# Twenty of the 64 chunks of w_down as seven block products in place of eight, and the transposes of q two half-chunks later

## The chip, the core and the metric

The kernel runs on one NeuronCore of a Trainium2 chip. The metric is the time of one execution on the device in microseconds (us); the median of three runs is compared. One further execution was recorded by the profiler.

TensorE multiplies matrices: it loads a 128x128 block as weights, streams up to 512 columns past it and adds the product to a bank of PSUM (eight banks of 128x512 fp32). VectorE and ScalarE work on tiles in SBUF and PSUM, GpSimd on tiles in SBUF. SyncE (SP) issues transfers. Each engine has a queue of its own and works through it in order; an instruction waits for the others by semaphores.

## What is computed

One decoder layer over 256 tokens of width 2048, in float32: a wide projection, a gated linear recurrence and sliding-window attention side by side, a mix, and a feed-forward part:

```
h = rmsnorm(x, norm_mix);  z = h @ w_in                  # 2048 x 9472
o_hg = hgrn2(...);  o_at = swa_sinks(rmsnorm(q), rmsnorm(k), v, sinks)
x = x + (sigmoid(g_hg) * (o_hg @ w_hg_out) + sigmoid(g_at) * (o_at @ w_at_out)) @ w_out
h2 = rmsnorm(x, norm_ffn)
x = x + square(relu(h2 @ w_up)) @ w_down                 # w_up 2048 x 8192, w_down 8192 x 2048
```

The change concerns the last product, and the transposes of the attention's q.

## The kernel before

All weights are read once, in 234 chunks of 1 MB (128 partitions x 16 x 128 values). A chunk `raw` is cut into two halves. A half is one *tick* of the program's main loop, so chunk i has the ticks 2i and 2i+1. For the accuracy of float32, each half is split into a rounded part `hi` (ScalarE's cast, `split_hi`) and the remainder `lo` (VectorE's subtraction, `split_lo`), and the activations are stored split in the same way. TensorE forms three products, of `hi` with `hi`, of `hi` with `lo` and of `lo` with `hi`.

The loop's order is the order of each engine's queue. At tick t it issues the cast of the half t+3, the remainder of the half t+2, the work that results due at t (`due`), then TensorE's matmuls of the half t, then what a table of ticks puts behind them (`post` for VectorE, ScalarE and GpSimd, `pe_side` for TensorE). A load is issued three chunks ahead. There are four buffers for `raw`, four for `hi` and three for `lo`.

The feed-forward part runs in two halves of D_FF. In each, 32 chunks of w_up give the activations `u0` and `u1` (16 tiles of 128 features x 256 tokens each, held as weights for the next product), and then 32 chunks of w_down follow. For w_down, a group of 8 chunks makes 512 columns of the output: `mm_tok` has 12 matmuls of 512 columns for each half chunk, six into the bank of the first 128 tokens and six into that of the other 128. `add_tok` then adds both banks to `x2`, which is the result; in the second half of D_FF it is written out at once.

`psm` and `pss` are two pools of four PSUM banks each. w_up and w_down use `psm`; `pss` holds small side results.

For q, `queries(b, tick)` takes one half of the heads: at `tick` it squares and sums (`a`), at tick+2 VectorE scales q (`a2`, the instruction written as aq<-aq,qsm, L714), at tick+3 TensorE makes eight transposes (`turn`, L724), at tick+4 ScalarE copies them out (`out`). The first half of q has tick 76, so its transposes stand behind the matmuls of tick 79. At tick 78, `post` also holds VectorE's products of the last recurrence group (L461, L462, L465), issued ahead of `a2`.

Of the kernel before, what the change touches and what calls it, by code (L numbers as in the profile page):

```python
# [18 lines left out]
P = 128  # L19
# [23 lines left out]
def trunk_kernel(  # L43
# [46 lines left out]
    rstd = base.tile([P, T], F32, name="rstd")  # L90
    keep = base.tile([P, T], F32, name="keep")
    consts = base.tile([P, C_W], F32, name="consts")
# [5 lines left out]
    sm = base.tile([P, 4, 2], F32, name="sm")  # L98
    qsm = base.tile([P, 3, 16], F32, name="qsm")
    base.tile([P, 232], F32, name="pad")  # L100

# [8 lines left out]

    raw_of, hi_of, lo_of = {}, {}, {}

    def load(i):
# [4 lines left out]
    def split_hi(h):  # L118
        i, q = divmod(h, 2)
        if N_START <= i < S_END:  # L120
            hi = hi_of[h] = split.tile([P, 8, P], F32R, tag="hi", bufs=4, name=f"hi{h}")
            nc.scalar.copy(hi, raw_of[i][:, 8 * q : 8 * q + 8, :])  # L122

    def split_lo(h):
        i, q = divmod(h, 2)
        if N_START <= i < S_END:
            lo = lo_of[h] = split.tile([P, 8, P], F32R, tag="lo", bufs=3, name=f"lo{h}")
            nc.vector.tensor_sub(lo, raw_of[i][:, 8 * q : 8 * q + 8, :], hi_of[h].bitcast(F32))  # L128
# [31 lines left out]
    def mm_tok(ps, act, k0, hi, lo, first, last):  # L160
        hi, lo = (w.rearrange("p (k a) b -> p k (a b)", k=2) for w in (hi, lo))
        for t in range(2):
            tok = slice(t * P, (t + 1) * P)
            for k in range(2):
                xh, xl = (act[:, k0 + k, a, tok] for a in range(2))
                nc.tensor.matmul(ps[t], lhsT=xh, rhs=hi[:, k, :], start=(first and k == 0), stop=False)  # L166
                nc.tensor.matmul(ps[t], lhsT=xh, rhs=lo[:, k, :], start=False, stop=False)  # L167
                nc.tensor.matmul(ps[t], lhsT=xl, rhs=hi[:, k, :], start=False, stop=(last and k == 1))  # L168

    def psum_main(i):  # L170
# [182 lines left out]
    def to_hgrn():  # L353
# [3 lines left out]
        for t in hg["aT"]:  # L357
            nc.gpsimd.memset(t, 0.0)
        nc.gpsimd.memset(keep, 1.0)
        nc.gpsimd.memset(keep.rearrange("p (c r) -> p c r", c=4)[:, :, 0:1], 0.0)  # L360
# [14 lines left out]
    def group(g):  # L375
# [55 lines left out]
        def post_scan():  # L431
            for i in range(2):
                v = st["lf"][:, i, :]
                nc.vector.tensor_tensor_scan(v, keep, v, 0.0, ALU.mult, ALU.add)  # L434

# [255 lines left out]
    def queries(b, tick):  # L691
# [10 lines left out]
        def a():  # L702
            sq = hg["pool"].tile([P, 16, 64], F32, tag="aqs", name=f"aqs_{b}")
            nc.scalar.activation(sq, heads(), AF.Square)
            v, r, t = st["small"] = [qsm[:, k, :] for k in range(3)]
            nc.vector.tensor_reduce(v.unsqueeze(2), sq, AX.X, ALU.add)
# [27 lines left out]
        at_post(tick + 2, a2)  # L734
        at_pe(tick + 3, turn)
        at_post(tick + 4, out)

# [161 lines left out]
    def open_ff():  # L899
# [5 lines left out]
        acts["h2"] = p.tile([P, KT, 2, T], F32R, name="h2")  # L905
        gp["sq"] = p.tile([P, 512], F32, name="sqt")
        gp["ss"] = p.tile([P, 2, 4], F32, name="ss")
        gp["r2"] = p.tile([P, 2], F32, name="r2")
# [52 lines left out]
    at_post(2 * S_FF + 4, lambda: norm_post("2"))  # L961

    def evac_up(k):
        box = {}
# [5 lines left out]
        def q(ps, n):  # L970
            nc.scalar.activation(box["s"], box["s"], AF.Square)  # L971
            split_act(acts[f"u{k // 16}"][:, k % 16], box["s"], nc.gpsimd.tensor_copy)

        return [(1, 0, f), (1, 1, q)]

    def evac_down(n, half):
        def f(ps, i):
            add_tok(ps, n)
            if half == 1:
                for t in range(2):  # L980
                    cols = slice(512 * n, 512 * n + 512)
                    nc.sync.dma_start(out[t, :, cols], gp["x2"][:, t, cols])

        return [(1, 0, f)]

# [16 lines left out]
    for half in range(2):  # L1002
        for k in range(32):
            jobs.append(("one", lambda: acts["h2"], evac_up(k)))
        for n in range(4):
            for c in range(8):
                jobs.append(
                    (
                        "tok",
                        lambda c=c: acts[f"u{c // 4}"],  # L1010
                        evac_down(n, half) if c == 7 else None,
                        4 * (c % 4),
                        c == 0,
                        c == 7,
                    )
                )
    assert len(jobs) == S_END
# [16 lines left out]
    for tick in range(2 * S_END + 2):  # L1034
# [10 lines left out]
        if tick == 2 * S_OUT + 3:  # L1045
            open_ff()
        split_hi(ticks[tick + 3])
        split_lo(ticks[tick + 2])
        for f in due.pop(tick, ()):
# [14 lines left out]
        elif i < S_END:  # L1064
            kind, act, ef = jobs[i][:3]
            if kind == "tok":
                k0, first, last = jobs[i][3:]
# [56 lines left out]
def _layout(inputs):  # L1124
# [39 lines left out]
    w_mix = np.concatenate([g["w_hg_out"].reshape(1024, D), g["w_at_out"].reshape(1024, D)[perm]], axis=0)  # L1164
    w_down = g["w_down"].reshape(2, D_FF // 2, D)
    w_down_t = np.concatenate([_rows(w_down[0]), _rows(w_down[1])], axis=0)
    cst, csr = _constants()
# [29 lines left out]
```

## Time and profile before

| | us |
|---|---|
| median of 3 runs (1353.06 to 1354.23) | 1353.5 |
| profiled execution, its own time | 1351.39 |
| its span, first to last instruction | 1349.6 |
| TensorE busy in it | 1336.0 |
| VectorE busy | 829.5 |
| ScalarE busy | 681.2 |
| GpSimd busy | 153.5 |

Busy time counts the stretches in which an engine has an instruction under way. Matmuls overlap, so the length of one is longer than the distance from one to the next. "Idle before" names the engine and line whose instruction ended the wait.

### The profile page before, as it was taken

Reading aid. Unit: us, or ns where it says so; the run is one execution under the profiler, and the core shown is the slowest. Engines: PE = TensorE matmul, PEld = TensorE weight load, DVE = VectorE, ACT = ScalarE, POOL = GpSimd, SP = SyncE. Lnnn points to the kernel's source line nnn. Section 1 sums busy time; section 2 is a strip of 40 time slices with the busy share of each in tenths; the row PEclk is TensorE's granted clock in tenths of the full one; section 3 lists DMA queues with packets and bytes.
Section 4 is the critical chain, followed back from the end, with each engine's and each line's share of the span. In section 5 each row is a group of like instructions: output and inputs, shape, how many; then the busy total and the mean of one; then the engine's idle time right before and its main releaser. Section 6 shows DMA issues by size and latency. Waiting matters only on the chain.

```text
span 1349.6 us, 17486 instructions
## 1 busy us (share of the span) xinstructions
PE 1336.0 (99%) x6776; PEld 1129.6 (84%) x6776; DVE 829.5 (61%) x989; ACT 681.2 (50%) x960; POOL 153.5 (11%) x163
## 2 busy tenths in 40 slices
PE   8999999999999999999999999999999999999998
PEld 7888888788888888888888888888888888888887
DVE  5767797676565567655766665444456666644443
ACT  7756576565666644454544444334344444433332
POOL 0332453100000001000000000000001111100000
PEclk9999999999999999999999999999999999999999
DMA  9655545455444555655555555555555555556661
GB/s 355 224 194 172 185 160 187 148 177 180 162 168 170 179 189 179 246 184 176 192 191 193 193 192 194 187 190 196 200 193 188 188 188 187 187 188 211 216 212 47
DMA packets 43331, 255.38 MB, mean 189 GB/s; under 512 B 4336, under 2 KB 10096, under 8 KB 13808
## 3 DMA queue, kind: packets, MB, share of 16 engines
q1 hardware_dynamic: 43104, 254.23, 54.9%
q8 instruction: 53, 0.87, 0.3%
q14 instruction: 30, 0.25, 0.0%
q10 hardware_dynamic: 144, 0.03, 0.0%
HBM read 252.15 MB, written 2.10 MB: 188 GB/s over the span
## 4 chain that ended last, share of the span: by engine, by line
PE 94%; DVE 2%; ACT 1%; issue 1%; DMA 1%; POOL 0%; SPq 0%; DVEq 0%; ACTq 0%; POOLq 0%
PE mm L136 23%; PE mm L166 19%; PE mm L167 19%; PE mm L168 19%; PE mm L145 12%; DVE lo L128 1%; DMA raw<-w_in_t 1%; PE pt L808 0%; PE po L823 0%; DVE lf L434 0%; PE s L754 0%; ACT hi L122 0%; PE o L530 0%; PE tr L931 0%; PE mt L884 0%
## 5 line engine op out<-in xcount | busy, mean ns | idle before, releaser
L128 DVE TENSOR_TENSOR lo<-raw,hi 128x1024 fp32r<-128x1024 f32 x460 | 582.1, 1268 | 421.5 <-PE mm L167 270.6
L122 ACT CAST hi<-raw 128x1024 fp32r<-128x1024 f32 x460 | 483.0, 1052 | 604.7 <-PE mm L168 380.3
L136 PE MATMUL mm<-h,hi 128*128 128x512 f32 x1024 | 305.9, 392 | 0.0
L136 PEld LDWEIGHTS mm<-h,hi 128*128 128x128 f32 x1024 | 187.9, 188 | 37.5
L145 PE MATMUL mm<-h,lo 128*128 128x256 f32 x1024 | 214.8, 281 | 0.0
L167 PE MATMUL mm<-lo,u 128*128 128x512 f32 x512 | 199.2, 389 | 0.0
L168 PE MATMUL mm<-hi,u 128*128 128x512 f32 x512 | 199.2, 389 | 0.0
L166 PE MATMUL mm<-hi,u 128*128 128x512 f32 x512 | 199.2, 389 | 0.0
L145 PEld LDWEIGHTS mm<-h,lo 128*128 128x128 f32 x1024 | 166.6, 190 | 5.0
L166 PE MATMUL mm<-hi,hT 128*128 128x512 f32 x384 | 152.7, 398 | 0.0
L167 PE MATMUL mm<-lo,hT 128*128 128x512 f32 x384 | 150.0, 391 | 0.7 <-DVE lo L128 0.7
L168 PE MATMUL mm<-hi,hT 128*128 128x512 f32 x384 | 149.6, 390 | 0.0
L167 PEld LDWEIGHTS mm<-lo,u 128*128 128x128 f32 x512 | 96.1, 188 | 20.1
L166 PEld LDWEIGHTS mm<-hi,u 128*128 128x128 f32 x512 | 96.1, 188 | 19.9
L168 PEld LDWEIGHTS mm<-hi,u 128*128 128x128 f32 x512 | 96.1, 188 | 19.8
L131 POOL CAST u<-s 128x256 fp32r<-128x256 f32 x64 | 44.1, 689 | 578.0 <-ACT s L971 578.0
L136 PE MATMUL mm<-hT,hi 128*128 128x512 f32 x352 | 88.4, 393 | 0.0
L166 PEld LDWEIGHTS mm<-hi,hT 128*128 128x128 f32 x384 | 72.2, 188 | 15.4 <-issue 1.4
L168 PEld LDWEIGHTS mm<-hi,hT 128*128 128x128 f32 x384 | 72.1, 188 | 15.4
L167 PEld LDWEIGHTS mm<-lo,hT 128*128 128x128 f32 x384 | 72.2, 188 | 14.8 <-DVE lo L128 1.1
L136 PEld LDWEIGHTS mm<-hT,hi 128*128 128x128 f32 x352 | 63.5, 189 | 11.6
L145 PEld LDWEIGHTS mm<-hT,lo 128*128 128x128 f32 x352 | 47.9, 190 | 4.2 <-DVE lo L128 0.8
(201 smaller groups left out, 1271.4 us busy)
## 6 DMA issues: line engine op xcount, KB each, us to landing
raw<-w_in_t SPq DMA_DIRECT2D x73, 1024.0 KB, 4.9
raw<-w_up_t SPq DMA_DIRECT2D x64, 1024.0 KB, 4.9
raw<-w_down_t SPq DMA_DIRECT2D x64, 1024.0 KB, 4.9
raw<-w_mix_t SPq DMA_DIRECT2D x16, 1024.0 KB, 4.9
raw<-w_out_t SPq DMA_DIRECT2D x16, 1024.0 KB, 4.9
xs<-x_tok SPq DMA_DIRECT2D x2, 1024.0 KB, 15.9
x<-x_tok SPq DMA_DIRECT2D x8, 256.0 KB, 6.4
out<-x SPq DMA_DIRECT2D x8, 256.0 KB, 2.8
```

The lines of the kernel that those rows point to most:

```text
L122: nc.scalar.copy(hi, raw_of[i][:, 8 * q : 8 * q + 8, :])
L128: nc.vector.tensor_sub(lo, raw_of[i][:, 8 * q : 8 * q + 8, :], hi_of[h].bitcast(F32))
L131: copy(dst[..., 0, :], src)
L136: nc.tensor.matmul(ps, lhsT=hi[:, k, :], rhs=act[:, k0 + k, :, :].rearrange("p a t -> p (a t)"), start=(first and k == 0), stop=False,)
L145: nc.tensor.matmul(ps[:, T : 2 * T], lhsT=lo[:, k, :], rhs=act[:, k0 + k, 0, :], start=False, stop=(last and k == hi.shape[1] - 1),)
L166: nc.tensor.matmul(ps[t], lhsT=xh, rhs=hi[:, k, :], start=(first and k == 0), stop=False)
L167: nc.tensor.matmul(ps[t], lhsT=xh, rhs=lo[:, k, :], start=False, stop=False)
L168: nc.tensor.matmul(ps[t], lhsT=xl, rhs=hi[:, k, :], start=False, stop=(last and k == 1))
```

## The change

Two blocks of 128 features and two of 512 output columns make a 2x2 problem: A11, A12, A21, A22 are the blocks of the activations (token half by feature block of 128) and B11, B12, B21, B22 those of w_down (feature block by 512 columns). The layout of w_down is changed on the host, so that one chunk holds the four B blocks, and a group is now 16 chunks that make 1024 columns. In five chunks of each group (0, 3, 6, 9 and 12; 20 of 64) the product is made by seven block products (Strassen's scheme, in the form with 4 sums of A and 4 of B), each of three matmuls; in the other chunks by eight, also three matmuls each (`mm_four`).

* A's sums are made while w_up is worked (`sums_up`), on 128x128 blocks.
* B's sums are made by VectorE in place, in `raw` (`seven_sums`), after the first half's `hi` and `lo` are taken; the second half's `hi` and `lo` are taken from the sums. The first half has three blocks to split, the second four. The casts of such a chunk's first half are issued a tick earlier.
* The products 1, 5, 6, 7 accumulate in the four banks of `psm` over the five chunks, the products 2, 3, 4 and all ordinary chunks in the four banks of `pss`. `down_tail` adds the first four up and into `x2` at the ticks 26 to 30 of the group, and `end` adds the banks 2, 3, 4, 8 at its tick 31. Before, a group of 8 chunks ended with two adds.
* There are six buffers for `hi` and five for `lo`. To make room, `keep` and `qsm` move into another pool, and the program's scratch for descriptors is made smaller.
* `turn` and `out` of `queries` come at tick+5 and tick+6.

```diff
+    SEVEN = (0, 3, 6, 9, 12)
+    S_DOWN = (S_FF + 32, S_FF + 96)
+    def pieces(h):
+        return ((2, 4), (0, 1)) if h % 2 == 0 else ((0, 2), (2, 4))
...
+    def seven_sums(i):
+        b11, b12, b22, b21 = (block(i, n, n + 1) for n in range(4))
+        nc.vector.tensor_sub(b22, b22, b12)
+        nc.vector.tensor_sub(b12, b12, b11)
+        nc.vector.tensor_add(b11, b22, b11)
+        nc.vector.tensor_sub(b21, b21, b11)
...
-        at_pe(tick + 3, turn)
-        at_post(tick + 4, out)
+        at_pe(tick + 5, turn)
+        at_post(tick + 6, out)
...
+    def sums_up(k, sa, sb):
...
+        nc.vector.tensor_add(f[:, 0, :], a21, a22)
+        nc.vector.tensor_sub(f[:, 1, :], f[:, 0, :], a11)
+        nc.vector.tensor_sub(f[:, 2, :], a11, a21)
+        nc.vector.tensor_sub(f[:, 3, :], a12, f[:, 1, :])
+        split_act(acts[f"u{k // 16}"][:, k % 16 - 1, :, P:T], f[:, 0, :])
+        us = gp["us"][:, m]
+        nc.scalar.copy(us[:, 0], f[:, 1:4, :])
+        nc.vector.tensor_sub(us[:, 1], f[:, 1:4, :], us[:, 0].bitcast(F32))
...
+    def mm_seven(h, c, n):
...
+        if h % 2 == 0:
+            todo = (("1", own(ka, t0), 1, 0), ("3", of(2), 0, 0), ("2", own(kb, t0), 0, 1))
+        else:
+            todo = (("6", of(0), 0, 0), ("5", own(ka, t1), 0, 1), ("7", of(1), 1, 0), ("4", own(kb, t1), 1, 1))
...
+        def a():
+            ps.update({k: down.pop(k) for k in "1567"})
+            nc.scalar.copy(gp["sq"], ps["1"])
+            nc.vector.tensor_add(cell(0, n), cell(0, n), ps["1"])
...
+        def end():
+            for key, t, m in (("2", 0, n), ("3", 0, n + 1), ("4", 1, n), ("8", 1, n + 1)):
+                nc.vector.tensor_add(cell(t, m), cell(t, m), down.pop(key))
+                if half == 1:
+                    nc.sync.dma_start(out[t, :, 512 * m : 512 * m + 512], cell(t, m))
+        for k, g in enumerate((a, b, c, d, f)):
+            at_post(tick + 2 * SEVEN[-1] + 2 + k, g)
+        at_post(tick + 31, end)
...
+        h2, h3, h4 = ticks[tick + 2 : tick + 5]
+        split_hi(h3)
+        if seven(h3 // 2) and h3 % 2 == 1:
+            seven_hi(h3)
+        if seven(h4 // 2) and h4 % 2 == 0:
+            seven_hi(h4)
+        split_lo(h2)
+        if seven(h2 // 2) and h2 % 2 == 1:
+            seven_lo(h2)
+        if seven(h3 // 2) and h3 % 2 == 0:
+            seven_lo(h3)
+            seven_sums(h3 // 2)
```

On TensorE, this is the place of the first half of q's transposes before the change (`aqt`; the number behind `hi` and `lo` is the half's, the last number only a buffer's):

```order
L166 MATMUL mm76_1_2246<-hi79_2238,hT_92 128x512
L167 MATMUL mm76_1_2246<-lo79_2273,hT_92 128x512
L168 MATMUL mm76_1_2246<-hi79_2238,hT_92 128x512
L724 MATMUL aqt_0_0_2338<-consts_83,aq_0_2242 128x128 x4
L724 MATMUL aqt_0_1_2343<-consts_83,aq_0_2242 128x128 x4
L166 MATMUL mm76_0_2245<-hi80_2271,hT_92 128x512
L167 MATMUL mm76_0_2245<-lo80_2293,hT_92 128x512
```

And with the change:

```order
L198 MATMUL mm76_1_2246<-lo81_2324,hT_90 128x512
L199 MATMUL mm76_1_2246<-hi81_2291,hT_90 128x512
L524 MATMUL a_3_2373<-qq_3_2307,kk_3_2308 64x64 x2
...
L535 MATMUL kst_3_2372<-consts_82,carry_3_2310 128x128 x2
L762 MATMUL aqt_0_0_2388<-consts_82,aq_0_2242 128x128 x4
L762 MATMUL aqt_0_1_2393<-consts_82,aq_0_2242 128x128 x4
L197 MATMUL mm76_0_2245<-hi82_2322,hT_90 128x512
```

They stood behind the half 79; now they stand behind the half 81 and the small matmuls of the last recurrence group, which follow that half.

On VectorE, this is the end of a group of w_down in the first half of D_FF with the change; 302 to 307 are ordinary halves, 308 and 309 the two halves of the next group's first chunk:

```order
L134 TENSOR_TENSOR lo308_2_7646<-raw154_7582,hi308_2_7624 128x1024
L134 TENSOR_TENSOR lo308_0_7648<-raw154_7582,hi308_0_7626 128x512
L139 TENSOR_TENSOR raw154_7582<-raw154_7582 128x512
L140 TENSOR_TENSOR raw154_7582<-raw154_7582 128x512
L141 TENSOR_TENSOR raw154_7582<-raw154_7582 128x512
L142 TENSOR_TENSOR raw154_7582<-raw154_7582 128x512
...
L134 TENSOR_TENSOR lo309_0_7689<-raw154_7582,hi309_0_7670 128x1024
L134 TENSOR_TENSOR lo309_2_7691<-raw154_7582,hi309_2_7672 128x1024
L1101 TENSOR_TENSOR x2_4797<-x2_4797,d276_2_7110 128x512
L1101 TENSOR_TENSOR x2_4797<-x2_4797,d276_3_7106 128x512
```

Before the change, the same place on VectorE's queue reads:

```order
L128 TENSOR_TENSOR lo308_7566<-raw154_7494,hi308_7546 128x1024
L128 TENSOR_TENSOR lo309_7582<-raw154_7494,hi309_7564 128x1024
L128 TENSOR_TENSOR lo310_7600<-raw155_7528,hi310_7580 128x1024
L916 TENSOR_TENSOR x2_4797<-x2_4797,mm292_0_7328 128x512
L916 TENSOR_TENSOR x2_4797<-x2_4797,mm292_1_7329 128x512
```

Two adds that stood behind the next group's third `lo` have become twelve, of which four (`end`, L1101; two are shown) stand behind the next group's first chunk, and eight stand between the `lo` from 304 on and that chunk's second half.

## Rows read from the trace of the kernel before

**Rows 1.** The page: span, TensorE's busy time, its granted clock in tenths, the chain.

```profile
span 1349.6 us, 17486 instructions
...
PE 1336.0 (99%) x6776; PEld 1129.6 (84%) x6776; DVE 829.5 (61%) x989; ACT 681.2 (50%) x960; POOL 153.5 (11%) x163
...
PEclk9999999999999999999999999999999999999999
...
PE 94%; DVE 2%; ACT 1%; issue 1%; DMA 1%; POOL 0%; SPq 0%; DVEq 0%; ACTq 0%; POOLq 0%
```

**Rows 2.** Busy time by stretch: q's transposes, w_up, w_down.

```profile
core 0: us, PE busy (x) PEld busy (x) DVE busy (x) ACT busy (x) POOL busy (x), PEclk, DMA share, GB/s
...
244.00:250.00 6.00, 2.68 (x16) 2.41 (x17) 5.37 (x7) 2.60 (x4) 2.09 (x4) 1.00 0.33 97
642.00:820.00 178.00, 178.00 (x1030) 156.97 (x1030) 121.17 (x172) 90.65 (x140) 13.16 (x31) 1.00 0.57 192
820.00:995.00 175.00, 175.00 (x776) 144.98 (x775) 84.38 (x75) 68.26 (x66) 0.41 (x1) 1.00 0.57 195
```

**Rows 3.** Groups of instructions by form: busy us, mean ns, idle before.

```profile
L128 DVE TENSOR_TENSOR lo<-raw,hi 128x1024 fp32r<-128x1024 f32 x460 | 582.1, 1268 | 421.5 <-PE mm L167 270.6 <-PE mm L145 100.3 <-issue 25.7
...
L167 PE MATMUL mm<-lo,u 128*128 128x512 f32 x512 | 199.2, 389 | 0.0
...
L916 DVE TENSOR_TENSOR x<-x,mm 128x512 f32<-128x512 f32 x24 | 15.4, 680 | 6.4 <-PE mm L168 6.4
...
L285 DVE TENSOR_TENSOR slo<-raw,shi 128x512 fp32r<-128x512 f32 x16 | 10.2, 686 | 5.5 <-ACT shi L284 5.5
...
L320 DVE SCALAR_TENSOR_TENSOR dg<-consts,r,dg 128x128 fp32r<-128x128 f32 x4 | 1.3, 352 | 0.9 <-ACT dg L319 0.9
```

**Rows 4.** TensorE in order of time at q's transposes: start, us, what.

```profile
243.59 0.39 PE L168 MATMUL mm<-hi,hT 128*128 128x512 f32 x1
247.32 1.06 PE L724 MATMUL aqt<-consts,aq 128*128 128x128 f32 x8 [3.34 <-DVE aq L714]
248.14 0.47 PE L166 MATMUL mm<-hi,hT 128*128 128x512 f32 x1
```

**Rows 5.** VectorE in order of time, same place.

```profile
241.48 1.23 DVE L128 TENSOR_TENSOR lo<-raw,hi 128x1024 fp32r<-128x1024 f32 x1 [0.59 <-ACT hi L122]
242.62 0.69 DVE L461 TENSOR_TENSOR qq<-z,d 128x512 f32<-128x512 f32 x1
243.22 1.23 DVE L462 TENSOR_TENSOR kk<-kf,en 128x512 f32<-128x512 f32 x1
...
244.98 0.42 DVE L195 SCALAR_TENSOR_TENSOR qsm<-qsm 128x16 f32<-128x16 f32 x1
245.44 0.33 DVE L196 SCALAR_TENSOR_TENSOR qsm<-qsm 128x16 f32<-128x16 f32 x1
245.80 1.38 DVE L714 TENSOR_TENSOR aq<-aq,qsm 128x1024 f32<-128x1024 f32 x1
247.10 2.35 DVE L128 TENSOR_TENSOR lo<-raw,hi 128x1024 fp32r<-128x1024 f32 x2
```

**Rows 6.** VectorE in order of time in w_down and at the kernel's end.

```profile
829.44 1.23 DVE L128 TENSOR_TENSOR lo<-raw,hi 128x1024 fp32r<-128x1024 f32 x1 [1.48 <-PE mm L167]
832.16 1.23 DVE L128 TENSOR_TENSOR lo<-raw,hi 128x1024 fp32r<-128x1024 f32 x1 [1.49 <-PE mm L167]
...
863.22 1.28 DVE L916 TENSOR_TENSOR x<-x,mm 128x512 f32<-128x512 f32 x2
864.80 1.22 DVE L128 TENSOR_TENSOR lo<-raw,hi 128x1024 fp32r<-128x1024 f32 x1 [0.30 <-issue]
...
1345.66 0.69 DVE L916 TENSOR_TENSOR x<-x,mm 128x512 f32<-128x512 f32 x1 [0.67 <-PE mm L168]
```

**Rows 7.** ScalarE in order of time in w_down.

```profile
829.65 1.06 ACT L122 CAST hi<-raw 128x1024 fp32r<-128x1024 f32 x1 [1.66 <-PE mm L168]
```

**Rows 8.** Transfers by tensor: count, size, us from issue to landing.

```profile
raw<-w_down_t SPq DMA_DIRECT2D x64, 1024.0 KB, 4.9
```

More of the change, by code (lines that the diff above doesn't have):

```diff
@@ L168, in mm_tok, with three @@
                 nc.tensor.matmul(ps[t], lhsT=xl, rhs=hi[:, k, :], start=False, stop=(last and k == 1))
+    def three(ps, xh, xl, hi, lo, first, last):
+        nc.tensor.matmul(ps, lhsT=xh, rhs=hi, start=first, stop=False)
+        nc.tensor.matmul(ps, lhsT=xh, rhs=lo, start=False, stop=False)
+        nc.tensor.matmul(ps, lhsT=xl, rhs=hi, start=False, stop=last)
     def psum_main(i):
@@ L433, in post_scan @@
                 v = st["lf"][:, i, :]
[L434 removed]
+                nc.vector.tensor_tensor_scan(v, hg["keep"], v, 0.0, ALU.mult, ALU.add)
         def chunked(t):
@@ L972, in q @@
             split_act(acts[f"u{k // 16}"][:, k % 16], box["s"], nc.gpsimd.tensor_copy)
+            if k // 2 in SEVEN:
+                kept[k % 2] = box["s"]
+                if k % 2:
+                    sums_up(k, kept[0], kept[1])
         return [(1, 0, f), (1, 1, q)]
[L976 to L984, printed above, removed]
+    down = {}
@@ new lines, in cell, with own, of @@
+    def cell(t, n):
+        return gp["x2"][:, t, 512 * n : 512 * n + 512]
+    def mm_seven(h, c, n):
+        u = acts[f"u{c // 8}"]
+        us = gp["us"][:, SEVEN.index(c)]
+        ka, kb = (2 * c) % 16, (2 * c + 1) % 16
+        t0, t1 = slice(0, P), slice(P, T)
+        def own(k, tok):
+            return u[:, k, 0, tok], u[:, k, 1, tok]
+        def of(m):
+            return us[:, 0, m, :], us[:, 1, m, :]
+        hi, lo = hi_of.pop(h), lo_of.pop(h)
+        if h % 2 == 0:
+            todo = (("1", own(ka, t0), 1, 0), ("3", of(2), 0, 0), ("2", own(kb, t0), 0, 1))
+        else:
+            todo = (("6", of(0), 0, 0), ("5", own(ka, t1), 0, 1), ("7", of(1), 1, 0), ("4", own(kb, t1), 1, 1))
+        for key, (xh, xl), p, b in todo:
+            first = key not in down
+            if first:
+                down[key] = psum_main(f"d{h}_{key}") if key in "1567" else psum_side(f"d{h}_{key}")
+            three(down[key], xh, xl, hi[p][:, b, :], lo[p][:, b, :], first, c == SEVEN[-1] and key in "1567")
@@ new lines, in mm_four @@
+    def mm_four(h, c, last):
+        u = acts[f"u{c // 8}"]
+        k = (2 * c + h % 2) % 16
+        hi, lo = (w.rearrange("p (n a) b -> p n (a b)", n=2) for w in (hi_of.pop(h), lo_of.pop(h)))
+        for t in range(2):
+            tok = slice(t * P, (t + 1) * P)
+            for n in range(2):
+                key = ("2", "3", "4", "8")[2 * t + n]
+                first = key not in down
+                if first:
+                    down[key] = psum_side(f"d{h}_{key}")
+                w = n if h % 2 == 0 else 1 - n
+                three(down[key], u[:, k, 0, tok], u[:, k, 1, tok], hi[:, w, :], lo[:, w, :], first, last)
@@ L986, in trunk_kernel @@
+    for half in range(2):
+        for m in range(2):
+            down_tail(2 * m, half, 2 * (S_DOWN[half] + 16 * m))
     jobs = []
@@ L1065, in trunk_kernel @@
             kind, act, ef = jobs[i][:3]
-            if kind == "tok":
+            if kind == "down":
+                c = jobs[i][3]
+                if seven(i):
+                    mm_seven(h, c, jobs[i][4])
+                else:
+                    mm_four(h, c, c == 15 and odd == 1)
+            elif kind == "tok":
                 k0, first, last = jobs[i][3:]
```

76 lines of the change are left out of this document (51 added, 25 removed).

## The prediction

> **What bounds the kernel now.** I read the summary lines first. TensorE is busy for 1336.0 of 1349.6 us, the chain that ended last runs through it for 94%, and its granted clock is at the full level in every slice [rows 1]. So the time is the sum of TensorE's matmuls plus 13.6 us in which it had none. Next I read the stretches. In one half of the w_down work (820 to 995 us) TensorE is busy for all 175 us, VectorE for 84.38 and ScalarE for 68.26, GpSimd for 0.41; while w_up is worked (642 to 820) VectorE has 121.17 of 178. The only long hole after the start is at 244 to 250, where TensorE has 2.68 of 6 us [rows 2].
>
> In w_down the two helpers wait for TensorE, not the other way round: a `lo` of 1.23 us starts every 2.72 us after 1.48 us of waiting for a matmul [rows 6], a `hi` of 1.06 us after 1.66 us of the same wait [rows 7]. A half chunk is 12 matmuls, so a matmul of 512 columns costs 2.72 / 12 = 0.227 us there. (The 389 ns of its group [rows 3] is the length of one, and neighbours overlap.) A matmul taken away is worth 0.227 us as long as the helpers keep this distance.
>
> **The change, part by part.**
>
> *Matmuls.* A seven-product chunk has 21 matmuls of 512 columns in place of 24. Twenty chunks lose 60: 60 x 0.227 = 13.6 us. The other 44 chunks keep 24, in another order. In the rows now, w_down's output bank changes every six matmuls; afterwards every three.
>
> *VectorE in a seven-product chunk.* It casts seven blocks' remainders, not four: three `lo` of 128x1024 and one of 128x512, 3 x 1.23 + 0.69 [rows 6, 3] = 4.38 us, and adds four 128x512 sums in place, each 0.68 by the nearest adds [rows 3], 2.72 us. With the next two ordinary chunks (four `lo`, 4.92) a cycle of three chunks costs it 12.0 us. TensorE needs 9 + 12 + 48 = 69 matmuls = 15.6 us for the cycle. VectorE has 3.6 us to spare; hidden, and it would cost if its operations grew by a third.
>
> *The chain inside such a chunk.* The second half's `hi` wait for the sums, and the sums for the first half's `lo`. With five `lo` buffers the second piece of the first half's `lo` can start when TensorE has finished the half four before it; from there to the second half's first matmul TensorE has 3 x 12 + 9 = 45 matmuls, 10.2 us. The chain is 0.69 + 2.72 + 1.06 (`hi`, [rows 7]) + 1.23 = 5.7 us, and the other `lo` that stand in VectorE's queue between are at most two, 2.5 us. Hidden with some 2 us left.
>
> *The end of a group (the four banks of the products 1, 5, 6, 7, then 2, 3, 4, 8).* This is where VectorE is fullest, because the sums of the next group's first chunk fall between the adds. I count from the moment TensorE has finished the first half of chunk 12, when VectorE can start the second `lo` that follows it. Until TensorE needs the bank of product 3 again it has 12 + 72 + 3 = 87 matmuls, 19.7 us. VectorE has before that: five ordinary `lo` (6.15), all of the next seven-product chunk (4.38 + 2.72), eight adds of the tail (5.44) and two of `end` (1.36): 20.05 us. It is late by 0.3 us before any hand-over; about two stand in the stretch (ScalarE's copy of bank 1 ahead of the first add, the release of the `lo` buffer), and a queue that had work showed a gap of 0.30 us after the adds [rows 6]. I take 0.3 + 2 x 0.3 = 0.9 us of waiting. It happens only where a second group follows in the same half, so twice: +1.8 us. At the other two ends w_up or nothing follows, and neither needs the four banks. Bounds: 0 where VectorE's neighbours overlap, as in the two `lo` that take 2.35 together [rows 5]; 1.8 us each, 3.6 in all, if each of these 23 operations also stands 0.04 behind the one before, as the small ones in [rows 5] do.
>
> *The last adds.* Now one add of 0.69 us follows the last matmul [rows 6]. Afterwards the banks close three matmuls apart (0.68), so three of the four adds lie beside matmuls and one follows. Zero; at worst the three others queue, +2.0.
>
> *w_up.* Every third chunk gets four 128x128 sums, two splits (128x128 and 128x384) and two ScalarE copies. VectorE pays at most 5 x 0.35 + 0.68 [rows 3] = 2.4 us, plus about 0.8 of waiting for ScalarE; in three chunks it has 3 x (178 - 121.17) / 32 = 5.3 us idle [rows 2]. Hidden. The first seven-product chunk of a half is prepared while w_up's last results are drained: ScalarE's `hi` of its second half stands ahead of the copy that frees w_up's sum, so VectorE waits for both. The six operations from the sums to the second `lo` fit with a few tenths to spare by these prices. Zero, at worst 0.5 twice.
>
> *Transfers.* The same 64 chunks of 1 MB, 4.9 us to landing [rows 8] in a chunk time of 5.4; a seven-product chunk's buffer is freed under a half later than now, with three chunks loaded ahead. In the last half, four output transfers instead of two stand in SP's queue ahead of a load which has three more halves until its first cast. Zero.
>
> *Buffers, scratch.* Six `hi` and five `lo` buffers in place of four and three let the helpers run further ahead, elsewhere too; I count nothing for it. The smaller scratch and the tiles that moved touch no instruction.
>
> *q's transposes.* Now TensorE waits 3.34 us for VectorE's `aq` before the first eight [rows 4]. VectorE has a backlog of two muls, the norm and `aq` to 247.1, and only behind these the next two `lo`, 2.35 us together [rows 5]. Two ticks later the transposes no longer wait. TensorE goes on at 243.8 with the half whose `lo` is done (241.48 + 1.23), and is through it at 246.5; its next half needs the first of those two `lo` for its second matmul, at 246.8, and gets it at 247.10 + 1.2 = 248.3, so with the hand-over it waits 1.6 us there. That is what becomes late next. Without the transposes the half that starts at 248.14 would have started at 243.8 + 0.8 for the eight transposes, so 3.5 us are given back and 1.6 taken: -1.9 us. Bounds: 0 if the wait moves whole, -3.5 if the deeper buffers bring VectorE forward.
>
> Sum: -13.6 + 1.8 - 1.9 = -13.7 us. The profiled execution took 1351.39 us for a span of 1349.6; it should become about 1337.7, its span 1335.9. The median of the three runs is 1353.5, 2.1 above the profiled one, so 1339.8.
>
> **A rule that speaks against it.** The banks change more often. In these rows six matmuls a bank run at 0.227 us with the clock at 1.00 [rows 2, 6], and I find no row with a lower one. The Trainium skill, in "TensorE: Matmul & The Clock Gate", section "A second HAM failure mode: psum-queue depth-cycling", tells of a kernel that cycled through banks, idled a little between its groups of matmuls, and had its clock moving between the two levels. No run here shows that. Worked as a mechanism of this kernel: if all 64 chunks ran at 1.2 in place of 2.4 GHz, their 1476 matmuls would cost 0.227 more each (an estimate, by doubling the spacing of [rows 6]), +335 us, and 4% of them would undo the gain.
>
> **Rivals.**
> *Hand-overs add up (1343 to 1351).* Each seven-product chunk crosses between ScalarE and VectorE twice more; if TensorE waits 0.2 to 0.5 us at each of 20, 4 to 10 us come back. For it: VectorE's order is fixed, and one late `lo` delays the rest. Against: about 2 us of room.
> *Nothing gained.* The 13.6 us go into waits at the group ends and first chunks: +3.4 us at each of four. That needs VectorE four times as late as I count. 1351 to 1356.
> *Slower: VectorE becomes the bound.* Its operations did stretch elsewhere when GpSimd worked beside them, and in place updates have no row here. A cycle takes 12.0 us; TensorE waits from 15.6, and the kernel is slower than before from 15.6 + 0.68 = 16.3, operations 36% longer. At 50% longer, 18.0, it loses 20 x 2.4 = 48 us and ends at 1386. Against: GpSimd has 0.41 us of 175 in w_down [rows 2], so little can stretch them.
> *Clock*, as above: from 1370 up.
>
> **How the numbers follow.** My forecast (waits of 0 to 5 us in all): 0.72, 1336 to 1343. Hand-overs: 0.13. Nothing gained: 0.05. VectorE the bound: 0.08; clock: 0.02. Both bounds in my favour give 1353.5 - 13.6 - 3.5 = 1336.4, a half us less if small holes close. For 8 in 10 I take 1335.5 to 1347: the forecast's cases and about two thirds of the hand-overs. About 0.2%, 2.7 us, is what a measurement here can tell from no change. Faster by more: 0.85; within: 0.05; slower: 0.10.
>
> **What would show it.** TensorE: 60 matmuls of 512 columns fewer in the w_down groups, 0.227 us apart, no hole inside a group, and one of 0 to 2 us at the first use of bank 3 in each second group, released by VectorE's add. VectorE: about 140 us busy in a half of w_down in place of 84 in 175, still waiting for TensorE once a cycle. At 244 to 250 no wait at the transposes, one of about 1.6 us at a matmul for `lo`. I am wrong if TensorE waits for `lo` or `hi` in most seven-product chunks, if the sums take clearly over 0.7 us each, or if the granted clock falls.

## The result: 1334.2 us, 19.2 us less than before

The changed kernel took 1334.2 us (median; 1334.17 to 1334.24), the kernel before 1353.4 beside it (1353.06 to 1354.23): 0.986 of the time, 95% interval 0.985 to 0.987. The prediction had 1339.8 with a range of 1335.5 to 1347.0. The direction was right; the gain was 5.5 us larger than predicted, and the time lies 1.3 us below the range.

The page of the changed kernel:

```profile
span 1332.4 us, 17469 instructions
...
PE 1322.5 (99%) x6716; PEld 1118.8 (84%) x6716; DVE 940.3 (71%) x1201; ACT 715.3 (54%) x1024; POOL 182.7 (14%) x163
...
PEclk9999999999999999999999999999999999999999
...
PE 93%; DVE 3%; ACT 2%; DMA 1%; issue 0%; SPq 0%; POOL 0%; DVEq 0%; ACTq 0%
```

Against [rows 1], TensorE has exactly 60 matmuls fewer and is busy for 13.5 us less, VectorE has 111 us more work, and the chain still runs through TensorE. The span fell by 17.2 us, 1349.6 to 1332.4; the median by 19.2. Those two numbers differ by 2.0 us, which is a finding of its own (below).

The stretches, to read against [rows 2] (TensorE reaches w_down at 814.5 now, at 818.5 before):

```profile
core 0: us, PE busy (x) PEld busy (x) DVE busy (x) ACT busy (x) POOL busy (x), PEclk, DMA share, GB/s
...
244.00:250.00 6.00, 5.40 (x43) 3.96 (x41) 5.54 (x5) 1.06 (x2) 0.00 (x0) 1.00 0.48 167
820.00:995.00 175.00, 175.00 (x788) 145.48 (x788) 137.56 (x152) 85.15 (x91) 0.82 (x1) 1.00 0.58 205
```

In w_down VectorE went from 84.38 to 137.56 us of 175, as forecast (about 140), and TensorE still has no hole there. At 244 to 250 its busy time doubled, from 2.68 to 5.40. What TensorE waited for in the whole span, by engine and line:

```profile
engine line waited for: us in total, times, longest us
PE mm L167 <- ACT shi L320: 5.1, 2, 4.5
PE mm L198 <- DVE lo L159: 0.6, 1, 0.6
```

Before, the same view has these besides the start:

```profile
PE aqt L724 <- DVE aq L714: 3.3, 1, 3.3
PE mm L167 <- DVE lo L128: 0.7, 1, 0.7
PE mm L145 <- DVE lo L128: 0.4, 1, 0.4
```

The first line of the changed kernel is its start, which before had too (5.2). The second is all that is left of the 3.34 us at q's transposes [rows 4] and of the two waits for `lo`. So 4.4 us of waiting became 0.6.

**Where the span's 17.2 us came from**, by the times at which TensorE starts things. From the first matmul of w_down to the last, with w_up's second half between, it took 526.75 us before (818.49 to 1345.24) and takes 513.44 (814.51 to 1327.95): 13.3. Before, then after:

```profile
818.49 0.39 PE L166 MATMUL mm<-hi,u 128*128 128x512 f32 x1
...
1345.24 0.39 PE L168 MATMUL mm<-hi,u 128*128 128x512 f32 x1
```

```profile
814.51 0.39 PE L202 MATMUL mmd<-hi,u 128*128 128x512 f32 x1
...
1327.95 0.39 PE L204 MATMUL d<-hi,u 128*128 128x512 f32 x1
```

Ahead of w_down it is 4.0 earlier (818.49 to 814.51): 3.8 of that are the waits just counted, and 0.1 stands already at the first weights (the second wait of the start ends at 14.08 in place of 14.19). The rest behind the last matmul is the same to 0.1 us (4.4 and 4.5).

The 13.3 are 0.3 short of 60 x 0.227 = 13.6, and the trace has the place. At the first seven-product chunk of the first half, two matmuls stand 0.38 and 0.34 us behind the one ahead in place of 0.227:

```profile
817.73 0.39 PE L204 MATMUL mmd<-hi,u 128*128 128x512 f32 x1
818.11 0.50 PE L202 MATMUL mmd<-hi,us 128*128 128x512 f32 x1
```

The bank that this product writes had held w_up's last sum, which VectorE takes out at 817.65 to 818.06 (L216). The view of waits doesn't count this hold-up, since a matmul's length of 0.39 us covers it: a wait in that view is short of the real delay by some 0.16 us.

### The profile page after: what moved, and what is told of

It is laid out like the page before. It is cut to its first block, busy times and chain, and to the rows that moved or that the text cites. A ratio compares the mean times of both kernels' runs of the same rounds, so it can differ in the third digit from the quotient of the medians.

```text
span 1332.4 us, 17469 instructions
## 1 busy us (share of the span) xinstructions
PE 1322.5 (99%) x6716; PEld 1118.8 (84%) x6716; DVE 940.3 (71%) x1201; ACT 715.3 (54%) x1024; POOL 182.7 (14%) x163
## 4 chain that ended last, share of the span: by engine, by line
PE 93%; DVE 3%; ACT 2%; DMA 1%; issue 0%; SPq 0%; POOL 0%; DVEq 0%; ACTq 0%
PE mm L167 23%; PE mm L176 12%; PE mm L197 10%; PE mm L198 10%; PE mm L199 10%; PE d L202 7%; PE d L204 7%; PE d L203 7%; PE mmd L202 1%; PE mmd L203 1%; PE mmd L204 1%; DMA raw<-w_in_t 1%; DVE lo L159 1%; ACT hi L153 1%; PE pt L846 0%
## 5 line engine op out<-in xcount | busy, mean ns | idle before, releaser
L159 DVE TENSOR_TENSOR lo<-raw,hi 128x1024 fp32r<-128x1024 f32 x420 | 523.6, 1266 | 67.3 <-ACT hi L153 26.0
L153 ACT CAST hi<-raw 128x1024 fp32r<-128x1024 f32 x420 | 432.6, 1049 | 118.7 <-PE mm L199 59.2
L203 PE MATMUL d<-lo,u 128*128 128x512 f32 x392 | 152.5, 389 | 0.0
L202 PE MATMUL d<-hi,u 128*128 128x512 f32 x392 | 152.5, 389 | 0.0
L204 PE MATMUL d<-hi,u 128*128 128x512 f32 x392 | 152.5, 389 | 0.0
L127 ACT CAST hi<-raw 128x1024 fp32r<-128x1024 f32 x80 | 73.3, 943 | 117.0 <-PE d L204 82.3
L162 POOL CAST u<-s 128x256 fp32r<-128x256 f32 x64 | 53.6, 838 | 562.7 <-ACT s L1025 558.4
L215 ACT COPY t<-mm 128x256 f32<-128x256 f32 x90 | 33.3, 373 | 155.9 <-PE mm L176 155.2
L134 DVE TENSOR_TENSOR lo<-raw,hi 128x1024 fp32r<-128x1024 f32 x80 | 87.0, 1099 | 33.9 <-PE d L203 22.7
L216 DVE TENSOR_TENSOR s<-mm,t 128x256 f32<-128x256 f32 x90 | 37.7, 421 | 99.9 <-ACT t L215 99.9
L204 PEld LDWEIGHTS d<-hi,u 128*128 128x128 f32 x392 | 73.6, 188 | 15.4
L203 PEld LDWEIGHTS d<-lo,u 128*128 128x128 f32 x392 | 73.6, 188 | 15.3
L202 PEld LDWEIGHTS d<-hi,u 128*128 128x128 f32 x392 | 73.6, 188 | 15.2
L197 PEld LDWEIGHTS mm<-hi,hT 128*128 128x128 f32 x384 | 72.2, 188 | 15.5 <-issue 1.4
```

Of the source, the lines that this page charges most:

```text
L127: nc.scalar.copy(hi, block(h // 2, a, b))
L134: nc.vector.tensor_sub(lo, block(h // 2, a, b), hi.bitcast(F32))
L202: nc.tensor.matmul(ps, lhsT=xh, rhs=hi, start=first, stop=False)
L203: nc.tensor.matmul(ps, lhsT=xh, rhs=lo, start=False, stop=False)
L204: nc.tensor.matmul(ps, lhsT=xl, rhs=hi, start=False, stop=last)
```

## The profile after, step by step

VectorE in a seven-product chunk (start, us, line and operation; in brackets the idle time ahead and what ended it):

```profile
838.00 0.69 DVE L134 TENSOR_TENSOR lo<-raw,hi 128x512 fp32r<-128x512 f32 x1 [1.50 <-PE d L203]
838.60 0.68 DVE L139 TENSOR_TENSOR raw<-raw 128x512 f32<-128x512 f32 x1
839.32 0.69 DVE L140 TENSOR_TENSOR raw<-raw 128x512 f32<-128x512 f32 x1
...
841.94 1.23 DVE L134 TENSOR_TENSOR lo<-raw,hi 128x1024 fp32r<-128x1024 f32 x1 [0.47 <-ACT hi L127]
843.45 1.22 DVE L134 TENSOR_TENSOR lo<-raw,hi 128x1024 fp32r<-128x1024 f32 x1 [0.28 <-PE d L203]
```

Each sum takes 0.69 and starts 0.72 behind the one it depends on; the forecast had 0.68. VectorE still waits for TensorE (`<-PE d`) once or twice in the cycle, so the chunk's time is set by TensorE.

The end of the first group, where the prediction expected a wait; first VectorE, then TensorE, for which no wait is shown:

```profile
890.37 0.69 DVE L134 TENSOR_TENSOR lo<-raw,hi 128x512 fp32r<-128x512 f32 x1 [1.27 <-PE d L203]
...
893.76 0.68 DVE L1093 TENSOR_TENSOR x<-x,sqt 128x512 f32<-128x512 f32 x1
894.36 0.68 DVE L1094 TENSOR_TENSOR x<-x,mmd 128x512 f32<-128x512 f32 x1
...
895.56 2.35 DVE L134 TENSOR_TENSOR lo<-raw,hi 128x1024 fp32r<-128x1024 f32 x2
897.83 2.47 DVE L1101 TENSOR_TENSOR x<-x,d 128x512 f32<-128x512 f32 x4
```

```profile
898.94 0.39 PE L204 MATMUL mmd<-hi,u 128*128 128x512 f32 x1
899.16 0.39 PE L202 MATMUL d<-hi,us 128*128 128x512 f32 x1
```

An add that doesn't depend on the one ahead starts 0.60 us after it though it is 0.68 long (four in 2.47), and two `lo` take 2.35. The first add of `end` (L1101) is done at about 897.83 + 0.69 = 898.5, and TensorE writes into its bank at 899.16. VectorE even stood idle for 1.27 us ahead of 890.37, until TensorE freed a `lo` buffer.

q's transposes in the changed kernel, TensorE and then VectorE, against [rows 4] and [rows 5]:

```profile
246.19 0.50 PE L198 MATMUL mm<-lo,hT 128*128 128x512 f32 x1 [0.60 <-DVE lo L159]
...
250.28 1.04 PE L762 MATMUL aqt<-consts,aq 128*128 128x128 f32 x8
```

```profile
243.62 1.38 DVE L752 TENSOR_TENSOR aq<-aq,qsm 128x1024 f32<-128x1024 f32 x1
244.93 4.61 DVE L159 TENSOR_TENSOR lo<-raw,hi 128x1024 fp32r<-128x1024 f32 x4
```

The transposes no longer wait, and the wait moved to a matmul for `lo`, as forecast, but it is 0.60 us and not 1.6. VectorE's `aq` starts at 243.62 where before had 245.80: VectorE is 2.2 us ahead.

## The experiments

Twelve kernels ran, in four groups; "before" ran beside each group (medians 1353.57, 1353.33, 1353.46 and 1352.78). Spans are those of profiled executions. The median of a kernel without a long hole lies 1.4 to 2.2 us above its span.

**The change in its parts.** Only the transposes, on the kernel before:

```diff
-        at_pe(tick + 3, turn)
-        at_post(tick + 4, out)
+        at_pe(tick + 5, turn)
+        at_post(tick + 6, out)
```

> The kernel before, with the transposes of q two ticks later and nothing else. Theory A (the hole at the transposes is worth its 3.3 us less a wait of 1.6 us at the next half's remainder, as predicted; and the plain runs of the kernel before, which are 2 us longer than its profiled one, are longer because of that same hole): span 1347.7, median about 1349.5, that is 3.9 below before. Theory B (the 2 us between plain and profiled runs have nothing to do with the hole): span 1347.7, median 1351.5. Theory C (the transposes alone give the whole 3.5 us): span 1346.1.

Measured: median 1349.67 (1349.26 to 1350.83), 0.9976 of before (0.9966 to 0.9986), span 1347.5. TensorE at that place:

```profile
248.11 0.50 PE L167 MATMUL mm<-lo,hT 128*128 128x512 f32 x1 [1.71 <-DVE lo L128]
252.18 1.04 PE L724 MATMUL aqt<-consts,aq 128*128 128x128 f32 x8
```

A wait of 3.34 became one of 1.71, so the wait moved as predicted and 1.6 us were gained there (the prediction had 1.9). The span fell by 2.1: this execution's start was 0.85 earlier (13.34 against 14.19), and 0.4 were lost again in a hold-up just ahead (240.2 to 241.0) that before doesn't have.

The other way round, the changed kernel with the transposes back at their old ticks:

> The changed kernel, with the transposes of q back at their old tick. Theory A (deeper buffers have brought VectorE forward by 2.2 us and TensorE by 1.1 there): a hole of 2.3 us at the transposes in place of a wait of 0.6, span 1334.1, median 1335.9, or 2 more if the plain runs lose beside such a hole too. Theory B (only the place of the transposes matters): the full hole of 3.3 us, span 1335.9 to 1336.

Measured: median 1336.71, 0.9877 (0.9863 to 0.989), span 1335.9. Its four executions took 1335.35, 1335.72, 1337.70 and 1337.73. The profiled one is among the long ones; TensorE in it, and the granted clock in two stretches:

```profile
245.22 1.06 PE L762 MATMUL aqt<-consts,aq 128*128 128x128 f32 x8 [2.50 <-DVE aq L752]
246.04 0.48 PE L197 MATMUL mm<-hi,hT 128*128 128x512 f32 x1
...
246.74 0.63 PE L199 MATMUL mm<-hi,hT 128*128 128x512 f32 x1
247.16 0.63 PE L197 MATMUL mm<-hi,hT 128*128 128x512 f32 x1
```

```profile
244.00:247.00 3.00, 1.78 (x11) 1.67 (x12) 3.00 (x3) 1.11 (x2) 0.00 (x0) 0.90 0.01 3
247.00:250.00 3.00, 3.00 (x8) 2.28 (x8) 2.62 (x3) 2.04 (x3) 0.00 (x0) 0.53 0.96 319
```

Behind a hole of 2.50 us matmuls stand 0.43 us apart in place of 0.227, with a granted clock of 0.53: the lower of the two levels, 1.2 in place of 2.4 GHz. It lasted for about eight matmuls and cost this execution some 2 us (1337.7 against 1335.4). The mean granted clock of the four, in the order above, is 1.000, 1.000, 0.998 and 0.999. The Trainium skill says the same in kind in "TensorE: Matmul & The Clock Gate", section "HAM oscillation — how this bites in real kernels": a stretch without matmuls sends the clock back to its lower level. Here two of the four executions were long.

Only the buffers, the moved tiles and the scratch, on the kernel before:

```diff
-            ... tag="hi", bufs=4 ...
+            ... tag="hi", bufs=6 ...
-            ... tag="lo", bufs=3 ...
+            ... tag="lo", bufs=5 ...
...
```

> The kernel before with only the deeper buffers (six hi, five lo, keep and qsm in the other pool, the smaller scratch). Theory A (ScalarE's casts were held up by the four hi buffers before its table load at 213 us, and everything behind it was late): the waits of 0.7 and 0.4 us of TensorE for lo between 140 and 230 us go, the hole at the transposes shrinks to 2.3 us, span 1347.5. Theory B (deeper buffers do nothing): span 1349.6, hole 3.3 us.

Measured: median 1350.43 (1349.13 to 1351.14), 0.9975 (0.9966 to 0.9984), span 1348.9. The wait at the transposes is 2.5 in place of 3.3 us, and of the 1.1 us of waits for `lo` elsewhere 0.2 are left. In this profiled execution, too, the clock fell behind the hole (0.82 at 244 to 247, 0.61 at 247 to 250). So these edits are worth something by themselves, where the prediction had counted nothing. Three things were edited together, but w_down takes its 526.75 us as before, so the moved tiles show no effect on it, and what changed are waits: on ScalarE the cast ahead of the table load no longer waits for a `hi` buffer, and `osqh` starts at 214.83 (for both see the rows at the end of the next section). That points to the buffers; the tiles and the scratch were not run alone.

Both together, still with the old w_down:

> The kernel before with both the deeper buffers and q's transposes two ticks later, w_down as it was. Theory A (these two make the whole gain ahead of w_down, the new grouping of w_down by 16 chunks and four banks costs and gains nothing): span 1345.4 and median 1347.1, as with the new grouping and no seven products. Theory B (the grouping gained part of it): span 1346 to 1347.

Measured: median 1347.09 (1346.7 to 1347.62), 0.9956 (0.9944 to 0.9969), span 1345.7; TensorE waits 0.6 us once for `lo`. And the changed kernel with every chunk by eight products, in its new grouping and banks, without the sums and without `down_tail`'s five steps:

```diff
     def seven(i):
-        return any(d <= i < d + 32 and (i - d) % 16 in SEVEN for d in S_DOWN)
+        return False
...
```

> The changed kernel with all 64 chunks of w_down by eight products (groups of 16 chunks, four banks, no sums, no tail of seven products), everything else as changed. Theory A (the seven products give 60 matmuls of 0.227 us and cost no wait at all): span 1332.4 + 13.6 = 1346.0, median 1347.8. Theory B (the seven products gave more, or less, than their matmuls, for instance a wait of 1.8 us at the group ends that is hidden in the total): span off 1346.0 by more than 1 us.

Measured: median 1347.09 (1346.96 to 1347.77), 0.9955 (0.9942 to 0.9969), span 1345.4. The two agree, so the new order of blocks and banks by itself costs and gains nothing; in both it is 526.75 us from w_down's first matmul to its last, as before. The seven products are the difference to the changed kernel: 12.9 us by the medians, 13.0 by the spans.

**Where the 2 us between the median and the profiled execution of before come from.** Before, with 12 unread matmuls in the hole at q:

```diff
+            if b == 0:
+                fill = psum_side("fill")
+                for _ in range(12):
+                    nc.tensor.matmul(fill, lhsT=ones, rhs=..., start=True, stop=True)
```

> The kernel before with twelve extra matmuls of 512 columns, whose result nobody reads, ahead of q's first transposes, where TensorE stood idle for 3.3 us. They take 12 x 0.227 = 2.7 us of the hole and move no other instruction. Theory A (the plain runs of the kernel before are longer than its profiled one because TensorE's granted clock falls behind this hole in most of them): median about 1351.4 with a spread under 1 us, though more work is done. Theory B (the 2 us come from something else): median 1353.5 and the spread of 3 us as before.

Measured: median 1351.76 (1350.94 to 1352.00, 11 executions), 0.9987 (0.9979 to 0.9996), span 1350.0. Before beside it spread from 1351.02 to 1354.73 (15 executions). TensorE:

```profile
243.99 2.88 PE L720 MATMUL fill<-hT,cr 128*128 128x512 f32 x12
247.76 1.06 PE L730 MATMUL aqt<-consts,aq 128*128 128x128 f32 x8 [0.88 <-DVE aq L714]
```

Work was added, the span rose by 0.4 us, and the median fell by 1.6 while the spread shrank to 1 us. So most executions of before lose about 2 us to something that the hole brings on, and with [rows 2] (clock 1.00 at 244 to 250) its profiled execution, 1351.39, was one that lost nothing. The rows of the two kernels above show what it is: the clock behind the hole. The record agrees, since it has the mean granted clock of every execution, not only of profiled ones. Of the 46 executions of before beside the experiments, the four under 1352.0 us have 0.999 or 1.000 and 34 of the other 42 have 0.997 or 0.998; with the hole filled all eleven have 0.999 or 1.000.

**The margin at the end of a group.** The changed kernel with extra additions ahead of the last four of each group, first four, then two:

```diff
+            for _ in range(4):
+                nc.vector.tensor_add(gp["sq"], gp["sq"], gp["sq"])
```

> The changed kernel with four more adds of 128x512 in each group's tail (at tick 30, on a scratch tile that nobody reads afterwards), each 0.72 us behind the one before. Theory A (at the end of a group VectorE just meets TensorE, with some 0.05 us left): TensorE waits about 2.8 us at the bank of product 3 in the second group of each half, twice, span 1338.0, median 1339.8. Theory B (VectorE has slack there, my count of its work is too high): less than 2 us in all, span under 1334.4.

Measured: median 1338.55 (1338.29 to 1340.63), 0.9897 (0.9882 to 0.9912), span 1337.0. The last adds start 2.69 us later and TensorE waits 2.02, twice; theory A had 2.8, so more than its 0.05 us was to spare:

```profile
901.26 0.50 PE L202 MATMUL d<-hi,us 128*128 128x512 f32 x1 [2.02 <-DVE x L1103]
```

> The changed kernel with two extra additions of 128x512 on VectorE ahead of the last four of each group of w_down (on a scratch tile that nothing else needs), where the run before had four. Theory A: the end of a group has a margin of about 0.65 us in the changed kernel, as the run with four showed (its last additions came 2.7 us later, TensorE waited 2.0 us). Two additions, 0.6 to 0.72 us each, put the end 1.2 to 1.4 us later: a wait of 0.6 to 0.8 us, twice, a span of 1333.6 to 1334.0 us and a median near 1335.6. Theory B, that there was no margin and a fixed loss of some other kind was hidden in the run with four: a wait of 1.2 to 1.4 us, twice, a span of 1334.8 to 1335.2. If the margin is over 1.4 us, no wait and a span of 1332.4.

Measured: median 1336.03 (1335.55 to 1336.51), 0.9873 (0.9857 to 0.989), span 1334.1. VectorE's last adds and TensorE's wait:

```profile
899.15 2.47 DVE L1103 TENSOR_TENSOR x<-x,d 128x512 f32<-128x512 f32 x4
```

```profile
899.88 0.50 PE L202 MATMUL d<-hi,us 128*128 128x512 f32 x1 [0.57 <-DVE x L1103]
```

They start 1.32 us later than in the changed kernel, and 0.57 is waited for. TensorE goes on 0.73 us after the adds begin (899.15 to 899.88), when the first of the four is done. In the changed kernel that moment is 897.83 + 0.73 = 898.56, and TensorE comes to the bank at 899.16: a margin of 0.6 us. (Lateness less wait gives 0.67 and 0.75 in the two runs; the view of waits is short by some 0.16.)

**More chunks by seven products.** Six of each sixteen in place of five (24 of 64):

```diff
-    SEVEN = (0, 3, 6, 9, 12)
+    SEVEN = (0, 2, 5, 7, 10, 12)
```

> The changed kernel with six seven-product chunks in each group of 16 (0, 2, 5, 7, 10, 12) in place of five, 24 of 64. Theory A (each costs TensorE nothing but its 21 matmuls): 4 x 3 x 0.227 = 2.7 us less, span 1329.7, median 1331.5. Theory B (with only one ordinary chunk between two of them VectorE, 9.3 us of work in 10.2, or the chain from the sums to the second half's remainder, comes too late): waits for lo at chunks 2, 7 and 12, 1 us or more each, 12 of them, span over 1333.

Measured: median 1331.97 (1331.78 to 1332.2), 0.9844 (0.9831 to 0.9858), span 1330.0, with 0.3 us of new waiting. It beats both kernels, by 2.2 us (medians) the changed one. Then seven of sixteen (28 of 64), for which two unused padding tiles had to go (the edit is against the changed kernel):

```diff
-    big.tile([P, 224], F32, name="pad0")
...
-    base.tile([P, 24], F32, name="pad")
...
-    SEVEN = (0, 3, 6, 9, 12)
+    SEVEN = (0, 2, 4, 6, 8, 10, 12)
...
-    ... dynamic_dma_scratch_size=1024)
+    ... dynamic_dma_scratch_size=512)
```

> The changed kernel with 28 of 64 chunks by seven block products in place of 20 (two more of each group of sixteen, so that the plain chunks that stand between two such ones fall away), with a scratch that is no longer padded. Theory A: TensorE is the only bound in w_down as long as VectorE's work for a chunk is shorter than TensorE's, and a seven-product chunk takes 12 x 0.227 = 2.7 us less of the matmuls; 24 of 64 measured 2.4 us below 20 of 64, so eight more chunks give 8 x 0.6 to 8 x 0.68 = 4.8 to 5.4 us, a span of about 1327.3 us (1332.4 less 5.1) and a median near 1329.1, with no wait for VectorE longer than 0.3 us. Theory B: VectorE is the next bound. Such a chunk gives it the casts' subtractions and four sums and TensorE 2.7 us less to cover them, and with no plain chunk between to catch up in, each later chunk of a group waits for lo: waits of 0.5 to 1.5 us at lo in four to eight chunks, which take back 2 to 8 us: a span of 1329.5 to 1335 and a median of 1331 to 1336.

(One chunk saves 3 x 0.227 = 0.68 us; the 2.7 in this text is what four save.) Measured: median 1336.75 (1336.05 to 1337.36), 0.9878 (0.9863 to 0.9893), span 1334.9: slower than with 20 or 24. Neither theory holds. TensorE does not wait for VectorE in w_down but for 0.4 us at the first seven-product chunk of each half, though VectorE works there almost without a break; it repeats every 9.62 us there, and TensorE takes 10.35 for the same two chunks:

```profile
829.13 2.35 DVE L157 TENSOR_TENSOR lo<-raw,hi 128x1024 fp32r<-128x1024 f32 x2
...
838.75 2.35 DVE L157 TENSOR_TENSOR lo<-raw,hi 128x1024 fp32r<-128x1024 f32 x2
```

Its 45 matmuls should take 10.2. Two more kernels, both with 24 chunks, told apart what had changed beside the count. Without the two padding tiles and with the smaller scratch:

> 24 of 64 chunks by seven products, as in the run of that name (span 1330.0 us, median 1331.97), but with the two unused padding tiles left out and the descriptor scratch halved again, as the kernel with 28 of 64 had them. In that kernel TensorE hardly waited, yet the distance of its matmuls in w_down was 0.230 us in place of 0.227, and 1.9 us were lost ahead of w_down. Theory A: the placement of the tiles in SBUF and the scratch cause both. Then this kernel, whose VectorE has as much room as with 24, shows matmuls 0.229 to 0.230 us apart in w_down and a later first matmul of w_down (816 us in place of 814.2): a span of about 1330.0 + 1.9 + 64 chunks x 22.9 x 0.002 to 0.003 = 1335 to 1336 us. Theory B: VectorE, which then works without a break in the first twelve chunks of each group, slows TensorE's matmuls. Then this kernel has them 0.227 us apart and a span of 1330.0 us, at most 1332 if the loss ahead of w_down is the scratch's.

Measured: median 1338.26 (1338.18 to 1338.33), 0.9892 (0.9877 to 0.9906), span 1336.4. Without the padding tiles alone:

> 24 of 64 chunks by seven products with the two unused padding tiles left out and the scratch as in the changed kernel. It tells the two halves of the run above apart. If the scratch causes the loss, this one is at a span of 1330.0 us, matmuls in w_down 0.227 us apart; if the placement of the tiles does, it is where the run above is, 1335 to 1336 us; if VectorE's unbroken work does, both are at 1330.0 us.

Measured: median 1338.73 (1338.21 to 1338.9), 0.9895 (0.9878 to 0.9911), span 1336.8. So it is the placement of the tiles, the only thing that this kernel changes against the one with 24 chunks above. With and without two tiles that no instruction touches, 896 and 96 bytes of each partition, the same program differs by 6.8 us, by the spans and by the medians. A group of matmuls (busy us, mean ns) with the tiles and without:

```profile
L203 PE MATMUL d<-lo,u 128*128 128x512 f32 x368 | 143.2, 389 | 0.0
```

```profile
L201 PE MATMUL d<-lo,u 128*128 128x512 f32 x368 | 143.8, 391 | 0.0
```

The first half's w_down took 166.2 us with them (814.15 to 980.34) and 167.8 without (816.24 to 984.04), the second half's 166.2 and 167.8 (1159.32 to 1325.49 and 1164.46 to 1332.29), and w_up between 1.4 more: 4.7 of the 6.8, at a granted clock of 1.00 and with no wait in it that the view shows. The matmuls just stand a little wider. A half of w_down has 732 of them here, and 1.6 to 1.7 us more make the distance 0.229 to 0.230 us in place of 0.227. Ahead of w_down 2.1 more are lost, 1.5 of them by 55 us; 0.7 of these stand by 31 us, where the start varies by as much from one execution to another (its second wait ends at 13.34 to 14.19 in kernels that have the tiles), so only the 4.7 are surely the placement's. The kernel with 28 chunks has the placement of the first of these two, and its span is 1.5 below that one's, of the 2.7 us that four more such chunks should bring. Which tiles collide, and with whose accesses, was not tried; nor was 28 with the old placement, for which there was no room.

## Why the prediction was right in sign and wrong in size

*Matmuls* (13.6): right. w_down shrank by 13.3 from first to last matmul, and 12.9 to 13.0 by the run without seven products. *VectorE in a seven-product chunk* and *the chain inside* were right too: no wait for `lo` or `hi` stands inside a group, and VectorE has its 137.56 us of 175. *Transfers* and *the last adds* cost nothing, to 0.1 us, as said. *w_up* ("Zero, at worst 0.5 twice") cost 0.3 once, at the bank of w_up's last sum (818.11). The granted clock stayed at 1.00 with the bank changing every three matmuls, so the clock rival fell; the idle time between groups of matmuls, of which the prediction's rule on bank cycling tells, doesn't occur here, so that rule as a whole is not tested. The rivals of hand-overs, of a VectorE bound and of nothing gained fell with the 13.3 and the list of waits. (The 1386 of the VectorE rival adds its 48 us to the profiled 1337.7; from the median it would be 1388.)

*The end of a group* (+1.8): mis-sized, it is 0. The prediction came to "late by 0.3 us before any hand-over" and took 0.9 of waiting. The runs show 0.6 us to spare. Two parts of the count were too long: operations that don't depend on each other start 0.60 apart (adds) and 1.13 to 1.17 (`lo`), where I took their lengths, 0.68 and 1.23; and it counted two adds of `end` ahead of the bank of product 3, where TensorE goes on after the first. Nor is the stretch one unbroken row of work, as the count had it: the wait of 1.27 us ahead of 890.37 stands in it. "0 where VectorE's neighbours overlap" was a bound of mine, and [rows 5] already had two `lo` in 2.35. The Trainium skill, in "VectorE: DVE Perf Modes", section "The DRAIN you can't avoid", says that a next operation that is not held starts earlier; the 0.60 agrees.

*Buffers, scratch* ("I count nothing for it") and *q's transposes* (-1.9): mis-sized together. Alone, the moved transposes turned a wait of 3.34 us into one of 1.71, as worked out. With the deeper buffers, VectorE's queue reached `aq` 2.2 us earlier and TensorE its half only 1.3 (the half 79 ends at 242.25 in place of 243.59, by the starts of the last matmuls), so the wait behind it is 0.60; and the waits for `lo` of 0.7 and 0.4 us elsewhere are gone. That made 3.8 us in place of 1.9. The run with both and the old w_down confirms it: its span is 3.9 below before. What runs ahead are ScalarE's casts. Before, ScalarE ahead of q:

```profile
209.52 0.37 ACT L523 COPY S<-kv 128x256 f32<-128x256 f32 x1
212.29 1.06 ACT L122 CAST hi<-raw 128x1024 fp32r<-128x1024 f32 x1 [2.39 <-PE mm L168]
213.37 1.28 ACT L401 ACT_TABLE_LOAD   x1
...
217.08 0.59 ACT L545 ACTIVATE osqh<-o 128x512 fp32r<-128x512 f32 x1
```

And after:

```profile
208.45 1.05 ACT L153 CAST hi<-raw 128x1024 fp32r<-128x1024 f32 x1
209.53 1.28 ACT L439 ACT_TABLE_LOAD   x1
...
215.01 0.60 ACT L583 ACTIVATE osqh<-o 128x512 fp32r<-128x512 f32 x1 [1.67 <-PE o L575]
```

A cast that waits for TensorE to free a `hi` buffer holds up everything queued behind it on ScalarE. Before, the matmuls whose result `osqh` reads were done at 216.3, and ScalarE came to it 0.75 us later; now they are done at 214.98 and ScalarE is already waiting for them. So of the 2.1 us by which `osqh` comes earlier (215.01 in place of 217.08), 1.3 are TensorE's, whose two waits for `lo` are gone, and the rest ScalarE's. VectorE, which waits for `osqh` (its copy L546, now L584, starts at 215.64 in place of 217.70), carries these 2.1 us on to `aq`. The prediction named the buffers and did not ask what stood behind the waiting cast; its sentence that the moved tiles "touch no instruction" held for this kernel (0.227 us before and after), but not for the one without the padding tiles.

*The offset* (+2.1): wrong in kind. "The median of the three runs is 1353.5, 2.1 above the profiled one" was carried over as a constant. It is the clock falling behind the 3.34 us hole in most executions of before, and not in the profiled one. With the hole gone, the changed kernel's profiled execution, 1334.2, is its median.

The sum of what was measured: 13.3 (w_down) + 3.8 (waits ahead of it) + 0.1 (start) = 17.2 of span, and 2.0 of the clock: 19.2. That the clock is behind the 2.0 is shown in the two kernels whose profiles fell into it, by the filled hole, and by the mean granted clock of before's long and short executions; where in a long execution of before the clock fell, no trace shows.

## What to carry to other kernels

Before a deeper buffer is costed at nothing, look for the instructions that wait for a buffer (a cast ended by a matmul), and ask what is queued behind them. Where the median lies above the profiled execution, find which hole brings that on before carrying the difference over: a change that closes the hole takes it away too. And count a queue's throughput by the distance from start to start in rows of neighbours, not by the length of one.

## What had not been expected of the hardware

After a hole of 2.5 us, TensorE's clock was at its lower level in some executions of a kernel and not in others (1335.4 against 1337.7 us for the same program), so one profile can miss it. Behind before's hole of 3.34 us the profiled execution shows 1.00 throughout.

The placement of tiles in SBUF moved TensorE's matmuls in w_down from 0.227 to 0.229 or 0.230 us apart, at full clock and without a wait that any view shows. With w_up between, that is 4.7 us of 1330 (6.8 with what is lost ahead of w_down), for 992 bytes of each partition that nothing reads. A kernel's own placement should be kept when something else is compared, and the distance of matmuls checked wherever it moves. All the kernels from before to 24 chunks with the padding tiles have 0.227.
